# A diffusion block on one Trainium2 core: the attention's value projections emitted between the heads of the delta rule's convolutions

## The chip, the core and the metric

The kernel runs on one NeuronCore of one Trainium2 chip. The engines named below are the matrix engine (PE, whose weight loads the profile lists apart as PEld), the vector engine (DVE), the scalar engine (ACT), GpSimd (POOL) and the queue that issues all DMAs (SP). The metric is the device time of one execution in microseconds. Three executions of the kernel before took 1300.95, 1306.34 and 1319.71 us, so the median is 1306.34 us.

## What is computed

Two layers work on 256 latent tokens (`x`) and 256 context tokens (`ctx`), 1024 wide. In each layer one input projection feeds two mixers: a neighbourhood attention with 8 heads of 64, and a gated delta rule with 4 heads of 128 that runs forwards and backwards over chunks. Both are joined by an output projection, and a squared-ReLU MLP follows. Cut to what matters here:

```python
nq, nk, nv, qkv, z, beta_raw, a_raw = jnp.split(h_lat @ w_in, cuts, axis=-1)      # and the same for the context
na_lat = neighbourhood_attention(heads(nq), heads(nk), heads(nv), ck_h, cv_h, rpb, rows)   # needs nv
q, k, v, beta, g = gdn_inputs(qkv, beta_raw, a_raw, conv_w, a_log, dt_bias, rope)  # conv of width 5, silu, l2norm
o_f, _ = gated_delta_chunked(q, k, v, g[:, :, 0], beta[:, :, 0], s_f)              # holds unit_lower_inverse(a)
y_lat = jnp.concatenate([na_lat, gated_rmsnorm(o_f + flip(o_b), z, gdn_norm_w)], axis=-1) @ w_out
```

The attention needs its values `nv` only when it multiplies by them. Nothing of the delta rule reads them.

## The kernel before

All 512 tokens are held on chip, and the weights stream in as 128x1024 blocks of 512 KB. A product of float32 quality is made of three matmuls on rounded halves (`mm3`, lines 274 to 276), so a weight block is first split: ACT writes the high half `whi` (line 248), DVE subtracts to get the low half `wlo` (line 250). `getw` hands out the blocks in the fixed sequence of `weight_order`, which is derived from the same strings as the program below; three split blocks are kept ahead.

The work of a layer's mixer is written as a string of letters, `CFG["ord0"]` and `CFG["ord1"]`, and `run_order` turns each letter into a call:

- `H` is `gdn_head`: three projections of a delta-rule head (tile `psg`, 24 matmuls each), each followed by the convolution on DVE (line 531, four instructions), a transpose to tokens (`gtr`, line 538); then norms, with a power on POOL (line 229), a scaling on DVE (line 567), and a transpose back (`gtb`, line 570).
- `N` is `proj_nv`: one value projection of two attention heads (tile `psv`, 24 matmuls), a copy on ACT (`vT`), four transposes on PE (`pvt`, line 588) and a copy on ACT into `nv`. On DVE it needs one `wlo`.
- `K` and `Q` are `proj_qk`: the key and query projections of two attention heads (tile `psn`, 24 matmuls each), split on ACT and DVE (lines 744 to 754). `a` is `attend`: scores (`pss`, lines 695 and 696), softmax, transposes (line 713) and the product with `nv` (line 716).
- `f` is `fill`: two of 36 steps of the modulation vectors (tile `adaps`, line 301), each with a DMA of 512 KB of `w_ada`. `Z` is a gate projection (`psz`), `B` and `C` are the decay gates.

At the `X` the function emits the delta rule itself: decay products (line 815), a blockwise triangular inverse by DVE alone (30 pairs at lines 830 and 832, between transposes at 823, 833 and 837), the joining of the blocks by small matmuls on PE (lines 848 to 870; tiles `p1`, `pz`, `p2`, `p3`), and the scan (from line 895). The letters behind `X` are emitted after that.

The letters set priorities only. A list scheduler of the compiler goes through the program, gives each engine its instructions by emission order among those that it holds ready, and fixes one order for each engine; on the chip every engine takes its instructions in that order. So work emitted late (value projections, `K`, `Q`, `a`, `f`) is drawn forward into holes that the scheduler sees on PE in the earlier stages.

Of the kernel before, what the change touches and what calls it, by code (L numbers as in the profile page):

```python
# [37 lines left out]
PAIR2 = True  # L38
KP_OUT = (2, 3, 0, 1)
CFG = {  # L40
    "ord0": "HHBHHCXfNffffNNfffffNKQffaaaKaQfaaKfaQfaffaaKfaQfaZaaaZZfffafffZ",
    "ord1": "BHHHHCNfffXNfffNfNfKfQfaafKfQfaaKfQKfaQfaafffZZZaZ", "tr": 7, "tr2": 2, "acc": 2, "g": 3, "n": 3,
    "late": 3, "tord": (0, 1, 2, 3), "adab": "n", "depth": 3, "npre": 8, "pre1": (0, 2, 3), "vt": "n",
    "tm": 1, "tmh": (2, 3), "gt": 2, "f02": 1, "f12": 2, "f13": 1,
    "start": "WLmmmWme01WLmmmm2eLmbm0mmbLe1m2m0mme12012bb", "cin": 7, "rows": 1,
# [1266 lines left out]
```

## Time and profile before

| | |
|---|---|
| executions shown | 1300.95, 1306.34 and 1319.71 us |
| the profiled execution's own time | 1319.72 us, of which its span is 1317.9 us |
| PE, DVE, ACT busy | 1260.9, 869.5, 594.7 us |
| mixer of layer 0, from its convolutions to its last attention | about 49.5 to 371 us of the span |
| mixer of layer 1 | about 819 to 1093 us |

A stretch of the program is called a stage below: the convolutions (until PE begins the gates' cumulative sums, line 641), the inversion stage (decay products and DVE's inverse, until PE's first `p1`), the block stage (until the first `pvn`, line 895), and scan and rest. Matmuls are pipelined and each is shown until its result is out, so that durations of neighbours overlap: 24 of 0.39 us each can fill 5.7 us.

### The profile page before, as it was taken

Reading aid. Unit: us, or ns where it says so; the run is one execution under the profiler, and the core shown is the slowest. Engines: PE = TensorE matmul, PEld = TensorE weight load, DVE = VectorE, ACT = ScalarE, POOL = GpSimd, SP = SyncE. Lnnn points to the kernel's source line nnn. Section 1 sums busy time; section 2 is a strip of 40 time slices with the busy share of each in tenths; the row PEclk is TensorE's granted clock in tenths of the full one; section 3 lists DMA queues with packets and bytes.
Section 4 is the critical chain, followed back from the end, with each engine's and each line's share of the span. In section 5 each row is a group of like instructions: output and inputs, shape, how many; then the busy total and the mean of one; then the engine's idle time right before and its main releaser. Section 6 shows DMA issues by size and latency. Waiting matters only on the chain.

```text
span 1317.9 us, 20437 instructions
## 1 busy us (share of the span) xinstructions
PE 1260.9 (96%) x7976; PEld 1003.5 (76%) x7976; DVE 869.5 (66%) x1679; ACT 594.7 (45%) x1063; POOL 81.3 (6%) x82
## 2 busy tenths in 40 slices
PE   6999999999999999999999999889989999899997
PEld 3676567877778987777788889665678877788996
DVE  3798795665479954344434588887853658866677
ACT  2555445654446622322322456554353455544542
POOL 0112000000101000000000001230000010000000
PEclk9999998999999999999999999999965999899999
DMA  9514552132165634533532345145710246555552
GB/s 327 207 64 149 179 181 66 45 108 86 61 212 200 212 117 127 158 114 127 158 118 96 112 163 205 61 152 173 237 59 21 89 143 233 188 188 191 180 189 96
DMA packets 62721, 190.93 MB, mean 145 GB/s; under 512 B 7808, under 2 KB 17824, under 8 KB 62624
## 3 DMA queue, kind: packets, MB, share of 16 engines
q1 hardware_dynamic: 62624, 189.62, 43.2%
q8 instruction: 63, 1.03, 0.3%
q14 instruction: 34, 0.28, 0.1%
HBM read 187.46 MB, written 2.13 MB: 144 GB/s over the span
## 4 chain that ended last, share of the span: by engine, by line
PE 74%; DVE 8%; ACT 3%; issue 3%; DMA 2%; POOL 1%; DVEq 0%; SPq 0%; ACTq 0%; POOLq 0%
PE pst L274 8%; PE pst L276 8%; PE pst L275 8%; PE pm L274 7%; PE pm L276 7%; PE pm L275 7%; PE pss L716 3%; PE adaps L301 3%; DMA wraw<-w_ada 2%; DVE wlo L250 2%; PE psn L274 2%; PE psn L275 2%; PE psn L276 1%; PE pss L696 1%; PE pss L713 1%
## 5 line engine op out<-in xcount | busy, mean ns | idle before, releaser
L250 DVE TENSOR_TENSOR wlo<-wraw,whi 128x1024 fp32r<-128x1024 f32 x224 | 272.8, 1220 | 195.1 <-ACT whi L248 194.5
L248 ACT ACTIVATE whi<-wraw 128x1024 fp32r<-128x1024 f32 x224 | 236.8, 1059 | 330.4 <-PE pst L276 169.9
L274 PE MATMUL pm<-hhi,whi 128*128 128x256 f32 (+1 forms) x544 | 176.7, 325 | 0.8 <-ACT whi L248 0.7
L276 PE MATMUL pm<-hhi,wlo 128*128 128x256 f32 (+1 forms) x544 | 175.0, 322 | 0.0
L275 PE MATMUL pm<-hlo,whi 128*128 128x256 f32 (+1 forms) x544 | 174.8, 321 | 0.0
L274 PE MATMUL pst<-whi,ah 128*128 128x512 f32 x384 | 151.9, 396 | 0.0
L275 PE MATMUL pst<-wlo,ah 128*128 128x512 f32 x384 | 151.3, 394 | 0.0
L276 PE MATMUL pst<-whi,al 128*128 128x512 f32 x384 | 151.1, 394 | 0.0
L274 PEld LDWEIGHTS pm<-hhi,whi 128*128 128x128 f32 x544 | 102.4, 188 | 15.2 <-issue 5.8
L276 PEld LDWEIGHTS pm<-hhi,wlo 128*128 128x128 f32 x544 | 102.4, 188 | 8.5
L275 PEld LDWEIGHTS pm<-hlo,whi 128*128 128x128 f32 x544 | 102.5, 188 | 8.1
L274 PEld LDWEIGHTS pst<-whi,ah 128*128 128x128 f32 x384 | 72.3, 188 | 17.1 <-issue 0.8
L276 PEld LDWEIGHTS pst<-whi,al 128*128 128x128 f32 x384 | 72.3, 188 | 16.8
L275 PEld LDWEIGHTS pst<-wlo,ah 128*128 128x128 f32 x384 | 72.3, 188 | 16.4
L274 PE MATMUL psg<-hhi,whi 128*128 128x512 f32 (+1 forms) x216 | 78.1, 363 | 4.0 <-ACT hhi L1067 1.9
L275 PE MATMUL psg<-hlo,whi 128*128 128x512 f32 (+1 forms) x216 | 77.9, 361 | 0.2 <-DVE hlo L1068 0.2
L276 PE MATMUL psg<-hhi,wlo 128*128 128x512 f32 (+1 forms) x216 | 77.3, 358 | 0.4 <-DVE wlo L250 0.4
L531 DVE SCALAR_TENSOR_TENSOR XT<-U,cw,XT 128x512 f32<-128x512 f32 (+1 forms) x96 | 67.0, 726 | 1.8 <-ACT XT L529 1.6
L1190 ACT ACTIVATE ah<-mr 128x256 fp32r<-128x256 f32 (+1 forms) x68 | 33.4, 491 | 66.2 <-DVE mr L1188 66.2
L301 PE MATMUL adaps<-wraw,scT 128*32 128x256 f32 x640 | 55.1, 391 | 3.8 <-DMA wraw<-w_ada 3.6
L274 PE MATMUL psn<-hhi,whi 128*128 128x512 f32 (+1 forms) x128 | 52.5, 410 | 0.0
L229 POOL TENSOR_TENSOR rs<-ve,mh 128x1 f32<-128x1 f32 x12 | 12.2, 1020 | 637.6 <-DVE bmv L394 368.4
(658 smaller groups left out, 2427.4 us busy)
## 6 DMA issues: line engine op xcount, KB each, us to landing
wraw<-w SPq DMA_DIRECT2D x140, 512.0 KB
wraw<-w_ada SPq DMA_DIRECT2D x80, 512.0 KB
wraw<-w_gdn SPq DMA_DIRECT2D x27, 512.0 KB
wraw<-w_out SPq DMA_DIRECT2D x24, 512.0 KB
xa<-w_ada SPq DMA_DIRECT2D x32, 256.0 KB
wraw<-w_vz SPq DMA_DIRECT2D x16, 512.0 KB
wraw<-w_na SPq DMA_DIRECT2D x16, 512.0 KB
lnrow<-lnr SPq DMA_DIRECT2D x8, 512.0 KB
```

The source lines that it names most:

```text
L229: G.tensor_tensor(outp, x, m, op=ALU.pow)
L248: S.activation(hi, r, AF.Copy)
L250: V.tensor_tensor(lo, r, hi.bitcast(F32), op=ALU.subtract)
L274: PE.matmul(o, l[0], r[0], start=start, stop=False)
L275: PE.matmul(o, l[0], r[1], start=False, stop=False)
L276: last_mm[:] = [PE.matmul(o, l[1], r[0], start=False, stop=stop).ins]
L301: PE.matmul(st["ps"][32 * g:32 * g + 32, :256], scT[:, k, :], w[:, 256 * g:256 * g + 256], start=(k == 0), stop=(k == 7), tile_position=(0 ...
L531: V.scalar_tensor_tensor(av, cin[:, sg:, kk:kk + 256], cw[:, b, kk:kk + 1], av, op0=ALU.mult, op1=ALU.add)
L696: PE.matmul(ps[:, :128 * nkt], nqT[hp][hs, a2, qs], nkT[hp][1][hs, :128 * nkt], start=False, stop=True)
L713: PE.transpose(ps[:, 128 * kt_:128 * kt_ + 128], p_[:, 128 * kt_:128 * kt_ + 128], ident)
L716: PE.matmul(ps[:, 0:65], p_[:, 128 * kt_:128 * kt_ + 128], nv[:, kt_, hd], start=kt_ == 0, stop=kt_ == nkt - 1)
L1190: S.activation(ah, r, AF.Copy)
```

## The change

The four `N` of each layer move from behind the gates (`C`) to places right behind the letters `H`. In layer 0 one `f` less stands in the string; the string had more `f` than there are steps, and what is left of the steps is emitted at its end, so the same steps run. No operation is added or removed.

```diff
-    "ord0": "HHBHHCXfNffffNNfffffNKQffaaaKaQfaaKfaQfaffaaKfaQfaZaaaZZfffafffZ",
-    "ord1": "BHHHHCNfffXNfffNfNfKfQfaafKfQfaaKfQKfaQfaafffZZZaZ", "tr": 7, "tr2": 2, "acc": 2, "g": 3, "n": 3,
+    "ord0": "HNHNBHNHNCXfffffffffKQffaaaKaQfaaKfaQfaffaaKfaQfaZaaaZZfffafffZ",
+    "ord1": "BHNHNHNHNCfffXfffffKfQfaafKfQfaaKfQKfaQfaafffZZZaZ", "tr": 7, "tr2": 2, "acc": 2, "g": 3, "n": 3,
```

What it does to the fixed orders of the engines is wider than that. Counted over PE's order of layer 0 (matmuls as the program issues them), stage by stage, before and after:

| layer 0, PE | `psv` | `psn` | `pvt` | `adaps` |
|---|---|---|---|---|
| convolutions | 35, 96 | 0, 4 | 4, 16 | 24, 5 |
| inversion stage | 61, 0 | 86, 137 | 12, 0 | 64, 91 |
| block stage | 0, 0 | 34, 3 | 0, 0 | 8, 0 |
| scan and rest | 0, 0 | 72, 48 | 0, 0 | 32, 32 |

In layer 1 the same counts are `psv` 37 and 96 in the convolutions, 59 and 0 in the inversion stage; `psn` 110 and 140 in the inversion stage, 43 and 4 in the block stage.

The first place is PE at the end of layer 0's convolutions, at the last head's transposes back (`gtb`). Before:

```order
L274 MATMUL psv_2139<-hhi_82,whi_1027 128x512
L301 MATMUL adaps_2030<-wraw_2100,scT_77 32x256 x4
L275 MATMUL psv_2139<-hlo_83,whi_1027 128x512
L276 MATMUL psv_2139<-hhi_82,wlo_1028 128x512
L274 MATMUL psv_2139<-hhi_82,whi_1027 128x512
L275 MATMUL psv_2139<-hlo_83,whi_1027 128x512
L570 MATMUL gtb_1012<-cst_63,ktok3_457 128x128 x4
L570 MATMUL gtb_1019<-cst_63,XT_447 128x128 x4
```

and now:

```order
L276 MATMUL psv_1193<-hhi_82,wlo_1077 128x512
L274 MATMUL psn_2309<-hhi_82,whi_1144 128x512
L275 MATMUL psn_2309<-hlo_83,whi_1144 128x512
L276 MATMUL psn_2309<-hhi_82,wlo_1145 128x512
L274 MATMUL psn_2309<-hhi_82,whi_1144 128x512
L588 MATMUL pvt_1220<-cst_63,vT_1218 128x128 x4
L301 MATMUL adaps_2186<-wraw_2187,scT_77 32x256
L570 MATMUL gtb_1129<-cst_63,ktok3_457 128x128 x4
```

Before, the second of the four value projections was under way at this point; now all four are done, and the first key projection has begun.

The second place is DVE inside layer 0's inverse, whose pairs are lines 830 and 832. Before:

```order
L830 TENSOR_TENSOR btmp<-MY 128x240
L832 TENSOR_TENSOR MY<-MY,btmp 128x15x16
L830 TENSOR_TENSOR btmp<-MY 128x238
L832 TENSOR_TENSOR MY<-MY,btmp 128x14x17
L250 TENSOR_TENSOR wlo<-wraw,whi 128x1024
L830 TENSOR_TENSOR btmp<-MY 128x234
L753 TENSOR_TENSOR KL<-psn,KS 64x512
```

and now:

```order
L745 SCALAR_TENSOR_TENSOR QS<-psn,QS 64x512
L832 TENSOR_TENSOR MY<-MY,btmp 128x22x9
L250 TENSOR_TENSOR wlo<-wraw,whi 128x1024
L830 TENSOR_TENSOR btmp<-MY 128x210
L250 TENSOR_TENSOR wlo<-wraw,whi 128x1024
L832 TENSOR_TENSOR MY<-MY,btmp 128x21x10
L745 SCALAR_TENSOR_TENSOR QS<-psn,QS 64x512
L830 TENSOR_TENSOR btmp<-MY 128x220
```

The queries of the first pair of heads now stand before step 11 of the inverse, where before the first keys came only behind step 17. Over the whole inverse (between the transposes at 823 and 833) DVE's order holds six `wlo` where it held four, four instructions each of lines 745, 753 and 754 where it held two each, and one more each of lines 307 and 710. In the decay products ahead of it there are no `wlo` where there were two. In layer 1 the inverse holds seven `wlo` for six and one more set of instructions for a score.

The third place is PE between the two halves of layer 0's first `p1`, the start of the block stage. Before:

```order
L274 MATMUL psn_2619<-hhi_82,whi_2357 128x512
L275 MATMUL psn_2619<-hlo_83,whi_2357 128x512
L276 MATMUL psn_2619<-hhi_82,wlo_2358 128x512
L301 MATMUL adaps_2261<-wraw_2649,scT_77 32x256 x4
L301 MATMUL adaps_2261<-wraw_2655,scT_77 32x256
L848 MATMUL p1_1308<-XT_447,U_446 32x32 x16
L852 MATMUL pz_1309<-U_446,y1_1307 32x32
```

and now:

```order
L276 MATMUL psn_2820<-hhi_82,wlo_2604 128x512
L848 MATMUL p1_1464<-XT_447,U_446 32x32 x16
L274 MATMUL psn_2820<-hhi_82,whi_2603 128x512
L275 MATMUL psn_2820<-hlo_83,whi_2603 128x512
L276 MATMUL psn_2820<-hhi_82,wlo_2604 128x512
L848 MATMUL p1_1464<-XT_447,U_446 32x32 x16
L852 MATMUL pz_1465<-U_446,y1_1463 32x32
```

Ten matmuls of a key projection and five of `adaps` stood between the halves; three matmuls stand there now.

## Rows read from the trace of the kernel before

**Rows 1.** The page: busy time of each engine; the span in 40 slices.
```profile
PE 1260.9 (96%) x7976; PEld 1003.5 (76%) x7976; DVE 869.5 (66%) x1679; ACT 594.7 (45%) x1063; POOL 81.3 (6%) x82
PEclk9999998999999999999999999999965999899999
```

**Rows 2.** Stages of both layers: stretch, its us, busy us (instructions), clock, DMA.
```profile
core 0: us, PE busy (x) PEld busy (x) DVE busy (x) ACT busy (x) POOL busy (x), PEclk, DMA share, GB/s
49.50:130.20 80.70, 73.39 (x387) 56.36 (x387) 72.29 (x144) 44.23 (x77) 19.78 (x21) 1.00 0.34 113
130.20:194.20 64.00, 60.52 (x364) 40.20 (x363) 51.78 (x108) 28.18 (x63) 3.51 (x1) 1.00 0.55 186
...
231.30:371.00 139.70, 137.99 (x886) 108.57 (x882) 78.23 (x234) 74.21 (x187) 12.32 (x11) 1.00 0.22 74
819.30:888.90 69.60, 61.08 (x356) 48.33 (x354) 61.02 (x138) 37.47 (x71) 17.51 (x20) 0.98 0.33 106
```

**Rows 3.** Waits of PE in the convolutions of layer 0, then of layer 1.
```profile
PE gtb L570 <- DVE ktok L567: 5.5, 4, 1.6
PE gtr L538 <- DVE XT L534: 1.7, 1, 1.7
...
PE gtb L570 <- DVE ktok L567: 4.5, 3, 1.5
PE adaps L301 <- DMA wraw<-w_ada: 1.9, 1, 1.9
PE psg L274 <- ACT XT L529: 1.3, 1, 1.3
PE gtr L538 <- DVE XT L534: 0.5, 1, 0.5
PE psg L276 <- DVE wlo L250: 0.4, 1, 0.4
```

**Rows 4.** One value projection on PE alone, 24 matmuls: us, busy PE, PEld, ACT, clock, DMA.
```profile
115.20:120.90 5.70, 5.70 (x24) 4.39 (x24) 0.00 (x0) 1.00 0.82 283
```

**Rows 5.** Groups on PE in layer 0's convolutions: busy us, mean ns, idle before.
```profile
L301 PE MATMUL adaps<-wraw,scT 128*32 128x256 f32 x48 | 3.8, 387 | 0.0
L588 PE MATMUL pvt<-cst,vT 128*128 128x128 f32 x4 | 0.6, 272 | 0.0
```

**Rows 6.** Groups on DVE in layer 0's inverse, 158.6 to 190 us.
```profile
L830 DVE TENSOR_TENSOR btmp<-MY 128x30 f32<-128x30 f32 (+14 forms) x30 | 9.9, 330 | 0.8
L250 DVE TENSOR_TENSOR wlo<-wraw,whi 128x1024 fp32r<-128x1024 f32 x4 | 4.9, 1221 | 0.2 <-ACT whi L248 0.2
L745 DVE SCALAR_TENSOR_TENSOR QS<-psn,QS 64x512 fp32r<-64x512 f32 x2 | 1.4, 688 | 0.1
L753 DVE TENSOR_TENSOR KL<-psn,KS 64x512 fp32r<-64x512 f32 x2 | 1.4, 684 | 0.0
L754 DVE CAST KS<-KS 64x512 fp32r<-64x512 f32 x2 | 0.8, 423 | 0.1
L825 DVE MEMSET MY<- 128x32 f32 x1 | 0.1, 85 | 1.2 <-ACT MY L824 1.2
```

**Rows 7.** PE in order of time where layer 0's block stage begins.
```profile
194.21 1.19 PE L848 MATMUL p<-XT,U 32*32 32x32 f32 x32 [1.85 <-ACT XT L835]
197.82 1.05 PE L301 MATMUL adaps<-wraw,scT 128*32 128x256 f32 x10
200.87 1.10 PE L848 MATMUL p<-XT,U 32*32 32x32 f32 x29 [2.00 <-ACT y L849]
```

**Rows 8.** The later part of the block stages, all instructions; columns as in Rows 2.
```profile
200.90:231.30 30.40, 30.40 (x546) 23.50 (x547) 15.20 (x37) 15.20 (x28) 0.00 (x0) 0.89 0.18 56
960.00:965.10 5.10, 2.77 (x16) 2.16 (x15) 4.99 (x7) 5.03 (x5) 0.00 (x0) 0.99 0.00 0
965.10:1013.00 47.90, 47.90 (x558) 39.73 (x558) 18.45 (x45) 18.10 (x33) 1.80 (x1) 0.50 0.14 42
```

**Rows 9.** The same two stretches, instructions on `psn` alone; busy PE, PEld, DVE, ACT.
```profile
200.90:231.30 30.40, 9.70 (x24) 5.67 (x24) 2.07 (x3) 1.71 (x3) 0.89 0.18 56
965.10:1013.00 47.90, 10.40 (x28) 6.98 (x28) 2.22 (x4) 1.94 (x4) 0.50 0.14 42
```

**Rows 10.** Stretch of the start with the highest DMA rate; PE's wait for DMA in layer 0's inversion.
```profile
20.00:40.00 20.00, 18.39 (x142) 9.35 (x141) 6.10 (x16) 3.68 (x7) 0.00 (x0) 1.00 1.08 365
...
PE adaps L301 <- DMA wraw<-w_ada: 1.5, 1, 1.5
```

## The prediction

> **What bounds the kernel now.** I read the page first. PE is busy for 1260.9 of 1317.9 us, and the clock line shows full speed nearly everywhere, with one dip to 0.6 and 0.5 in the second layer's mixer [rows 1]. Since the change adds no work, the time can only change through what PE waits for, and through the clock at which its work runs. So I cut the two mixers into stages and read the stretches one by one.
>
> In layer 0's convolutions both PE and DVE are nearly full: 73.4 and 72.3 of 80.7 us [rows 2]. PE waits 7.2 us there, 5.5 of them in four waits of `gtb` (one per head) for DVE's scaling, which itself stands behind a power on POOL [rows 3]. Layer 1 shows the same, with 8.6 us of waits [rows 3]. The reader is to see that there are holes, but that all of them together are half of one layer's moved work. In the inversion stage PE is busy 60.5 of 64.0 us, because projections and modulation steps fill the time in which DVE alone works at the inverse [rows 2]. The inverse itself leaves DVE hardly a gap: its 30 steps and all that stands between them follow each other, and the only large hole is 1.2 us in front of line 825 [rows 6]. The block stage begins with two waits of PE, 1.85 and 2.00 us, for ACT [rows 7], and is then full of PE work [rows 8]. What follows it is PE work without holes: 138.0 of 139.7 us [rows 2].
>
> **The change, step by step.** All sums are made against the profiled execution, 1319.7 us.
>
> *Unit prices.* 24 matmuls of a projection take 5.70 us when nothing disturbs them, so one is 0.238 us [rows 4]. Four `pvt` take 0.6 us, so one is 0.15. 48 records of `adaps` take 3.8 us [rows 5]; the program issues 24 there, so one issued is 0.158 us. A `wlo` is 1.22 us [rows 6].
>
> *Layer 0, convolutions.* PE gets 61 `psv`, 4 `psn` and 12 `pvt` more and 19 `adaps` less: 65 x 0.238 + 12 x 0.15 - 19 x 0.158 = 15.5 + 1.8 - 3.0 = 14.3 us. DVE gets three `wlo` more, 3.7 us, so by DVE the stage would end 3.7 us later and by PE more; PE sets the end. What PE gains is its waits. The first `gtb` comes where it came, since the instructions ahead of it on DVE are the same and PE has no more to do before it. Behind it PE has 74 to 96 projection matmuls per head where it had 53 to 74, and it reaches the later `gtb` after DVE. So I take off three of the four waits: 5.5 less the longest, 1.6, is 3.9. The stage ends **10.4 us later**. The bounds are 7.1 (all waits of PE go) and 14.3 (none goes).
>
> *Layer 0, inversion stage.* PE has 10 projection matmuls less and 27 `adaps` more, 12 `pvt` less: nearly the same work. DVE decides. Its inverse now holds two `wlo` (2.4), two of each of lines 753, 754 and 745 (1.4 + 0.8 + 1.4) and two short ones (0.8) more, 6.8 us [rows 6], and DVE takes its instructions in order, so they delay the steps behind them; `p1` on PE waits for the result. The two keys' instructions in front of line 825 fall into the 1.2 us hole. **5.6 us later**; bounds 0 (they fall into waits that the old trace does not show) and 6.8. The two `wlo` that leave the decay products fill holes there and give nothing back.
>
> *Layer 0, block stage.* Up to 200.9 us DVE and ACT set the pace; with three matmuls for ten between the halves of `p1` PE only waits longer. After that 24 `psn` and three `adaps` are gone, which took 9.7 + 0.5 us of a 30.4 us stretch that was full [rows 8, 9]. They covered the round trips from PE over ACT or DVE and back, of which the one that shows uncovered costs 2.0 us [rows 7]. I let two of these appear: 10.2 - 4.2 = **6.0 us earlier**; bounds 0 and 10.2.
>
> *Layer 0, scan and rest.* 24 `psn` and a few pieces of attention less on a full PE: 5.7 + 1 = **6.7 us earlier**. Layer 0 in all: 10.4 + 5.6 - 6.0 - 6.7 = +3.3.
>
> *Layer 1.* Convolutions: 63 projection matmuls and 12 `pvt` more, 7 `adaps` less: 15.0 + 1.8 - 1.1 = 15.7; here a whole value projection stands in front of the first `gtb`, so all its waits but the 1.3 for ACT go [rows 3]: 7.3 less, **+8.4** (bounds 7.1 and 15.7). DVE's two more `wlo` (2.4) are hidden under that. Inverse: one `wlo` and one score more on DVE, 2.3 at most; **+2** (bounds 0 and 2.3). Block stage: 28 `psn` of 10.4 us are gone, which ran at clock 0.50 [rows 8, 9], and about 2 us of attention; three of that come back as waits: **-9.4** (bounds 0 and -12.4). Rest: five `psn` more, **+1**. Layer 1: +2.0.
>
> *Sum.* 1319.7 + 3.3 + 2.0 = 1325. The profiled execution is 13.4 us slower than the median. [...] Then the sum is +10.0, from the median 1316. Which of the two the median is, one trace can't show; I take the middle, **1320 us**.
>
> *DMA.* No transfer is added. The 512 KB loads of `w_ada` move forward: 91 issued matmuls are 23 loads in layer 0's inversion stage for 16. 186 GB/s over 64 us are 11.9 MB; 3.7 MB more in 69.6 us make 224 GB/s, under the 365 that the start shows [rows 2, 10]. I put nothing on it; it is a rival below.
>
> *A rule weighed.* In the convolutions PE's matmuls are busy 91% of the time and its weight loads 56.4 of 80.7 us, 70% [rows 2]. [...] By that share alone 24 us would be free in the stage, and the value projections would cost only DVE's 3.7. In the stretch where PE runs one projection without a hole, however, the weight loads are 4.39 of 5.70 us, 77% [rows 4]; 70% of 77% is again 91%, so I keep 10.4.
>
> **The rivals.** *PE's clock falls in layer 0's block stage too.* In layer 1 PE was busy 2.77 of 5.10 us at 960 us, and from then to the first `pvn` the granted clock was 0.50; in layer 0, after waits of 1.85 and 2.00 us, it was 0.89 over the stage [rows 7, 8]. [...] Since part is hidden under the new waits I price it at 12: **1332**. [...]
>
> *The convolutions absorb the projections.* If PE has slack that the busy time hides, or if all waits go, DVE sets the end: 3.7 and 2.4 for 10.4 and 8.4, 12.7 less, **1307**, no slower than before. The sum of unit prices speaks against: 251 matmuls at 0.238, the transposes and the waits leave about 3 us of the 80.7. It decides where PE reaches each `gtb` before DVE.
>
> *The loads of `w_ada` come too late.* Such a wait costs 1.5 and 1.9 us [rows 10, 3]; seven loads more in layer 0 and two in layer 1 stand close behind each other, and PE takes them in order between the decay products. Five waits of 1.6: **1328**. The rate above speaks against it.
>
> That the projections stay where they were can't be: PE's fixed order has all four ahead of the last `gtb`.
>
> **How the numbers follow.** Forecast 0.45, 1312 to 1327; clock 0.25, 1328 to 1338; absorbed 0.18, 1299 to 1312; loads 0.12, 1322 to 1334. Together they put about 0.1 below 1303 and 0.1 above 1336, which is the range. 2% of 1306.34 is 26 us, about what a measurement of this kernel can tell from no change. Above 1332.5 lies about half of the clock's case and a quarter of the loads': 0.16. Below 1280 lies 0.03; the rest is 0.81.
>
> **What would show it.** In the profile after, the convolutions of layer 0 should last about 91 us with one large wait at `gtb`; the inverse between lines 825 and 833 about 5 us longer; PE should stand still for over 4 us between the halves of the first `p1`; the stretch from there to `pvn` should be about 24 us, and the clock line tells the second case. The prediction is wrong where the convolutions end within 4 us of before, or where the inverse is no longer than it was.

## The result, and the profile after

The changed kernel takes 1364.79 us (median of four executions, 1361.81 to 1365.54); the kernel before, on the same chip, 1312.94 us. The ratio is 1.04 with a 95% interval of 1.0341 to 1.0459: **slower by 52 us**. The forecast was 1320 us with a range of 1303 to 1336, so the measured time lies 29 us above the range.

The profiled execution's span is 1362.5 us for 1317.9, 44.6 us more. The two lines of the page that answer to [rows 1]:

```profile
PE 1289.3 (95%) x7976; PEld 1023.7 (75%) x7976; DVE 873.0 (64%) x1679; ACT 596.2 (44%) x1063; POOL 83.8 (6%) x82
PEclk9999977599999999999999999999875999899999
```

The same 7976 matmul records are busy for 28.4 us more: the work is the same, so part of it ran slower. The clock line has a new dip, 7 7 5, in layer 0's mixer. The stages of the changed kernel, columns as in [rows 2]: first layer 0's convolutions, inversion stage, block stage, scan and rest, then the same of layer 1.

```profile
49.50:144.90 95.40, 88.32 (x425) 69.48 (x423) 78.75 (x146) 50.28 (x85) 21.80 (x21) 0.98 0.25 81
144.90:220.00 75.10, 68.45 (x404) 40.99 (x403) 55.50 (x116) 27.02 (x60) 3.51 (x1) 0.91 0.66 209
220.00:264.50 44.50, 40.84 (x558) 33.57 (x558) 18.25 (x41) 20.00 (x30) 0.00 (x0) 0.51 0.04 10
264.50:399.20 134.70, 133.13 (x846) 105.39 (x844) 74.84 (x224) 71.44 (x183) 12.24 (x11) 0.97 0.21 70
847.80:931.90 84.10, 76.40 (x420) 61.96 (x420) 66.02 (x141) 43.69 (x80) 19.13 (x20) 0.98 0.27 85
931.90:1009.10 77.20, 64.35 (x410) 39.26 (x410) 56.46 (x127) 29.27 (x64) 3.51 (x1) 0.91 0.63 207
1009.10:1054.30 45.20, 39.30 (x553) 32.88 (x553) 20.18 (x41) 20.41 (x31) 1.80 (x1) 0.50 0.04 10
1054.30:1137.40 83.10, 82.57 (x603) 69.47 (x602) 46.29 (x146) 39.87 (x104) 7.58 (x8) 0.96 0.31 101
```

[rows 2] has four stages of the kernel before; the other four, layer 0's block stage and layer 1's last three, are:

```profile
194.20:231.30 37.10, 35.10 (x598) 26.80 (x599) 21.82 (x42) 21.83 (x32) 0.00 (x0) 0.91 0.18 58
...
888.90:958.40 69.50, 66.50 (x424) 42.92 (x423) 56.15 (x122) 31.40 (x68) 3.51 (x1) 1.00 0.63 203
958.40:1013.00 54.60, 52.25 (x605) 43.39 (x605) 25.05 (x51) 24.73 (x37) 1.80 (x1) 0.56 0.12 37
1013.00:1093.00 80.00, 79.88 (x600) 67.06 (x599) 47.76 (x145) 39.61 (x104) 7.60 (x8) 0.98 0.34 105
```

Layer 0's block stage now runs at a granted clock of 0.51 where it had 0.91, and PE stands for 12.85 us of layer 1's inversion stage (77.20 less 64.35) where it stood for 3.0.

**An account that closes.** Moved work adds nothing to a kernel whose bound is PE. It can only change how long PE stands, and how much of PE's work runs at the lower of the two clocks that these traces show, 0.50 and 1.00 of full speed: cut into slices of 1 us from 8 to 1317 us, the trace before has 70 at 0.50, 1227 at 1.00 and 12 between, the trace after 139, 1152 and 18. So I split each span into three: idle time (span less PE's busy time), half of what PE was busy in the stretches at half clock, and what is left, the work at full clock. The stretches at half clock that matter, and the sum over all of them, in the kernel before:

```profile
965.00:1016.20 51.20, 51.14 (x572) 42.98 (x573) 19.66 (x48) 19.65 (x40) 1.80 (x1) 0.50 0.13 40
...
sum 76.40, PE 69.32 PEld 55.87 DVE 37.32 ACT 29.83 POOL 2.39; mean PE 9.90 PEld 7.98 DVE 5.33 ACT 4.26 POOL 0.34
```

and in the changed kernel (layer 0's inversion stage, its block stage, layer 1's end of the inversion stage with its block stage):

```profile
179.90:193.60 13.70, 11.18 (x43) 5.53 (x44) 8.26 (x17) 3.13 (x6) 0.00 (x0) 0.50 0.64 197
220.90:268.70 47.80, 44.15 (x555) 36.88 (x553) 19.68 (x46) 21.89 (x39) 1.81 (x1) 0.50 0.03 10
...
1002.50:1060.60 58.10, 45.63 (x580) 39.12 (x581) 28.44 (x59) 24.69 (x39) 1.80 (x1) 0.50 0.07 21
...
sum 151.80, PE 125.60 PEld 101.53 DVE 79.55 ACT 58.29 POOL 6.02; mean PE 12.56 PEld 10.15 DVE 7.95 ACT 5.83 POOL 0.60
```

| us | before | after | difference |
|---|---|---|---|
| idle time of PE | 57.0 | 73.2 | +16.2 |
| half of the busy time at half clock | 34.7 | 62.8 | +28.1 |
| the rest: work at full clock | 1226.2 | 1226.5 | +0.3 |
| span | 1317.9 | 1362.5 | +44.6 |

The rest agrees to 0.3 us, so **28 us of the loss are clock and 16 us are PE standing**. By stage the 28 are 5.6 in layer 0's inversion stage, 18.7 about its block stage (44.15 less the 6.8 that two short dips had there before, halved), nothing in layer 1, and some 4 in dips of 3.4 us. The 16 are 3.2 in layer 0's inversion stage, 9.9 in layer 1's, 1.7 and 3.6 in the two block stages, and about -2 in the rest.

This is the split of two single executions. That the clock is lower is no accident of this pair: the mean granted clock over a whole execution was 0.944 to 0.949 in the four of the changed kernel, and 0.961 to 0.988 in those of the kernel before that the experiments were measured against.

What the convolutions didn't give back stands in their waits (us in total, times, longest); these answer to [rows 3], PE's in layer 0, then in layer 1:

```profile
PE gtb L570 <- DVE ktok L567: 5.0, 4, 1.5
...
PE gtb L570 <- DVE ktok L567: 5.9, 4, 1.6
```

and this is the wait of DVE that stands ahead of PE's in layer 0:

```profile
DVE grs L563 <- POOL grs L229: 5.1, 4, 1.6
```

All four waits of layer 0 are still there, 5.0 us for 5.5, and layer 1 has 5.9 for 4.5.

### The profile page after: what moved, and what is told of

Its sections match the earlier page's. It is cut to its first block, busy times and chain, and to the rows that moved or that the text cites. A ratio compares the mean times of both kernels' runs of the same rounds, so it can differ in the third digit from the quotient of the medians.

```text
span 1362.5 us, 20425 instructions
## 1 busy us (share of the span) xinstructions
PE 1289.3 (95%) x7976; PEld 1023.7 (75%) x7976; DVE 873.0 (64%) x1679; ACT 596.2 (44%) x1063; POOL 83.8 (6%) x82
## 3 DMA queue, kind: packets, MB, share of 16 engines
q1 hardware_dynamic: 62624, 189.62, 42.5%
## 5 line engine op out<-in xcount | busy, mean ns | idle before, releaser
L274 PEld LDWEIGHTS pm<-hhi,whi 128*128 128x128 f32 x544 | 102.4, 188 | 15.3 <-issue 5.8
L301 PE MATMUL adaps<-wraw,scT 128*32 128x256 f32 x640 | 59.8, 398 | 0.0
L276 PE MATMUL psn<-hhi,wlo 128*128 128x512 f32 (+1 forms) x128 | 52.2, 408 | 3.9 <-DVE wlo L250 3.9
```

The costliest lines, as they stand in the source:

```text
L274: PE.matmul(o, l[0], r[0], start=start, stop=False)
L276: last_mm[:] = [PE.matmul(o, l[1], r[0], start=False, stop=stop).ins]
L301: PE.matmul(st["ps"][32 * g:32 * g + 32, :256], scT[:, k, :], w[:, 256 * g:256 * g + 256], start=(k == 0), stop=(k == 7), tile_position=(0 ...
```

## The experiments

In the account used below, "idle" and "clock" are the first two rows of the table above for the run's profiled execution. Ratios are to the kernel before on the same chip; the changed kernel's is 1.04. The edits are cut to the lines that matter.

### One layer at a time

```diff
# e1_layer0: the kernel before with the new ord0 alone
+    "ord0": "HNHNBHNHNCXfffffffffKQffaaaKaQfaaKfaQfaffaaKfaQfaZaaaZZfffafffZ",
# e2_layer1: the kernel before with the new ord1 alone
+    "ord1": "BHNHNHNHNCfffXfffffKfQfaafKfQfaaKfQKfaQfaafffZZZaZ",
```

> Layer 0 alone takes the new order; layer 1 keeps the old one. If each layer's loss is made inside its own mixer, this run is slower than before by what the two profiles show between the starts of the two layers, about 28 us: +14 in the convolutions, +11 in the inversion stage, +7 in the block stage at a granted clock of 0.5, -5 in what follows. If the prediction's terms hold and the rest of the loss comes from the two layers disturbing one another (loads, or the clock of one stage carried into another), it is +3.

> Layer 1 alone takes the new order. If each layer's loss is its own, +16 us: +14 in the convolutions, +8 in the inversion stage, -9 in the block stage (which runs at a granted clock of 0.5 in either order), +3 in what follows. By the prediction's terms it is +2. The sum of this run and of the one with layer 0 alone should be the whole loss, about 45, if nothing couples the layers.

Layer 0 alone: 1336.41 us, ratio 1.0199 (1.0147 to 1.0251). Layer 1 alone: 1338.02 us, 1.0217 (1.0157 to 1.0277). Together 24.6 + 26.2 = 51 us is the whole loss, so each layer makes a loss by itself, and no large coupling shows. That the sum fits to 1 us is luck: each interval is some 7 us wide to either side, and the clock of the untouched layer moves by as much. Layer 1's share was expected at 16. Its own stages are as in the changed kernel (83.4, 76.4 and 42.8 us); what is more lies in the untouched layer 0, whose block stage fell to half clock in this execution:

```profile
194.10:241.20 47.10, 46.67 (x598) 35.23 (x598) 22.07 (x42) 21.91 (x32) 0.00 (x0) 0.64 0.15 46
```

The same instructions in the same order took 37.1 us at 0.91 in the trace that I predicted from. In the run with layer 0 alone it is layer 1's untouched block stage that differs, 42.8 us for 54.6. So the kernel before gets more than one clock pattern, and the one trace was no fixed number for either stage. With the old order of layer 0 untouched, its block stage also took 35.5 us at 0.90 (e13) and 47.1 us at 0.64 (e12). The executions of the kernel before over all batches lie between 1300.6 and 1328.7 us.

### Needless matmuls where the clock falls

```diff
# e3_after_fill (changed kernel, 12 per layer), e4_before_fill (kernel before, 8 per layer)
+    with tc.issue_after(p1_):          # behind the first half of the first p1
+        for _ in range(12):
+            PE.matmul(pz, hT[0][:, 0, 0:128], hT[0][:, 1, :], start=True, stop=True)
# e9_after_bigfill (changed kernel): 14 there, and four ahead of each p2 and p3
# e12_before_fill1 (kernel before, layer 1 alone): 14 there, and two ahead of each p2 and p3
```

> The changed kernel with 12 needless matmuls of 128x512 per layer behind the first half of the first p1, on operands that are there and into a tile that is overwritten before it is read: PE's work there is longer by about 12 x 0.24 = 3 us, and PE doesn't stand still between the halves. Nothing is left out of the computation. If the hole at the start of the block stage is what lets the clock fall, layer 0's block stage goes back to a clock near 1 and lasts some 30 us for 44.5, and the time falls by 10 to 14 us in layer 0, and by as much in layer 1 if the clock holds there too. If the clock has fallen for what lies ahead of the block stage (the half-idle inversion stage), the stage stays at 0.5 and the time is the same or 1 to 3 us longer. If the clock were the whole of the loss, the time would come back to within 15 us of before; by the stages' table it can't, since 14 + 11 us of layer 0 lie ahead of that stage.

> The kernel before with 8 such needless matmuls in the same place of both layers. In layer 1 the granted clock was 0.5 from the start of the block stage to the first pvn, 47.9 us. If the hole there is the cause, that stage shortens to 30 to 37 us and the kernel is 10 to 16 us faster than before; layer 0's stage, which was at 0.9, gets at most 2 us longer. If the cause lies ahead of the hole, no change, or 2 to 4 us slower by the work added.

> The changed kernel with 14 needless matmuls of 128x512 behind the first half of the first p1 and four before each p2 and p3 (46 a layer, 10.9 us at 0.238). In the changed kernel the block stage holds three psn and otherwise small matmuls, and runs at a granted clock of 0.5 for 38 us. If it is the missing large matmuls that keep the clock down, it comes back to near 1 within the stage: 38 us of work at half clock are about 20 at full clock, 11 of fill come on top, so the stage lasts 35 to 40 us for 44.5, and the kernel is 5 to 15 us faster than the changed one in spite of the work added. If the clock stays at 0.5 whatever PE does there, the stage lasts about 60 us and the kernel is 25 to 40 us slower.

> The kernel before with 30 needless matmuls of 128x512 in layer 1's block stage alone (14 behind the first half of the first p1, two before each p2 and p3; 7.1 us at 0.238). The account of the traces so far is: span = 1230 us of matmul work at full clock + half of the busy time at half clock + idle time. Before, layer 1's block stage is at half clock for 51 us, which costs about 21. If the fill keeps the clock, that falls to 5 to 10 and the kernel is 4 to 9 us faster than before; if the clock falls at the hole anyway and comes back no earlier, it is 7 to 14 us slower.

e3: 1358.66 us, ratio 1.0362 (1.0307 to 1.0416), not to be told from the changed kernel. The fill shortened PE's wait for ACT in the hole from 3.6 to 0.5 us, the clock came back for 6.8 us and fell again, and the stage lasted 42.4 us for 44.5. The hole alone isn't the cause. e4: 1330.23 us, 1.0138 (1.0069 to 1.0207), a little slower: the scheduler let the eight matmuls take the place of five psn and all five adaps in the hole, so PE waited there as before (2.3 us), and layer 0's stage had a half-clock stretch of 30.7 us.

e9 puts large matmuls through the whole stage. 1361.12 us, 1.0409 (1.0353 to 1.0465): the same as the changed kernel with 92 matmuls more, 21.9 us at 0.238. Layer 0's half-clock stretches are now

```profile
219.90:223.30 3.40, 3.40 (x8) 2.64 (x9) 3.35 (x3) 3.38 (x3) 0.00 (x0) 0.50 0.02 5
240.40:264.30 23.90, 23.90 (x246) 19.29 (x243) 5.41 (x14) 7.36 (x18) 0.00 (x0) 0.50 0.01 1
```

27.3 us for 47.8. The account has 39.6 us of clock for 62.8, and the mean clock was 0.964 to 0.970 in all four executions for 0.944 to 0.949: the fill earned back its own price and no more. Large matmuls in the stage shorten the time at half clock, so the loss of psn there (34 before, 3 after) is part of why it is long; as the clock fell again at 240.4 with PE busy throughout (40.24 of the stage's 40.70 us), they aren't all of it. e12, 1320.60 us, 1.0079 (1.0035 to 1.0124), shortened layer 1's block stage from 54.6 to 37.6 us, but layer 0's fell to half clock in its profiled execution, and the kernel was no faster.

### The waits at `gtb`

```diff
# e5_after_defer, e6_before_defer: gtb emitted behind the next head's first projection
-    PE.transpose(pb[:, t], tk[kind][:, t], ident)        # in gdn_head
+    pend.append((h, kind, q0, tk[kind]))                 # flushed behind the next psg
# e10_after_nopow, e11_before_nopow: no power on POOL
-    rsq(rs, ss, mh.rearrange("p (a b) -> p a b", a=2))
+    V.tensor_scalar(rs, ss, 0.05, None, op0=ALU.min)
# e14_before_split, e15_after_split: the power per projection, as soon as its sums are there
+    V.tensor_scalar(ss[:, kind], ss[:, kind], 4 * NORM_EPS, None, op0=ALU.add)
+    rsq(rs[:, kind], ss[:, kind], mh[:, 0:4])
```

> The changed kernel with the transposes back to channels (gtb) of each head emitted behind the next head's first projection (the last head's behind the gates), so that PE reaches them 15 to 20 projection matmuls, some 4 us, later. The four waits at gtb, 5.0 us in layer 0 and 5.9 in layer 1, should go. If PE's work sets the end of the convolutions and those waits are the whole of the slack, layer 0's stage ends 3.5 to 5 us earlier (from 96 to 91 or 92) and layer 1's 4 to 6 earlier, and the kernel is 8 to 11 us faster than the changed one. If DVE's chain sets the end (its own waits for split weights, 5.9 us, stand in it), the stage doesn't shorten: the waits only move to gtr or psg.

> The same edit on the kernel before, without the change. If PE sets the end there too, 5.5 us of waits go in layer 0 and 4.5 in layer 1: 6 to 10 us faster than before. If DVE, which is busy 72.3 of 80.7 us there, sets the end, no gain.

> The changed kernel with the power on POOL that scales the keys and queries of a head replaced by a small DVE instruction (a minimum with 0.05), so this part of the computation is changed: keys and queries aren't normalised. In the changed kernel DVE waits 5.1 us for that power in layer 0's convolutions, once per head, and PE waits 5.0 us at gtb, once per head. If the round trip over POOL is what keeps PE waiting at gtb, both go, and the convolutions end 4 to 5 us earlier in each layer: 8 to 10 us faster than the changed kernel. If DVE's chain as a whole is late, the wait at gtb or at gtr stays at 5 to 7 us per layer and the gain is under 4 us.

> The same replacement in the kernel before (keys and queries aren't normalised). If the round trip over POOL is the cause, the 5.5 and 4.5 us at gtb go and the kernel is 8 to 10 us faster than before; if DVE's chain as a whole is late, under 4 us.

> The kernel before with the power on POOL issued per projection, the key's as soon as its sums of squares are there, so that its round trip lies under the query's convolution. Same results, one small power and one small addition more per head. If the round trip is what keeps PE at gtb, most of the 5.5 and 4.5 us of waits go in the two layers and the idle time of PE falls from 57 to about 49; at equal clock the kernel is 6 to 9 us faster. If the query's own round trip still sets the wait, idle stays above 54 and the time is the same.

> The same edit on the changed kernel: gtb waits of 5.0 and 5.9 us go for the most part, convolutions of layer 0 end 3 to 5 us earlier (from 96 to about 92), and the kernel is 6 to 10 us faster than the changed one, still 30 or more slower than before.

e5: 1359.64 us, 1.040 (1.035 to 1.045), no gain. Layer 0's `gtb` waits are gone, and PE waits at the next transpose of the chain, `gtr`, instead:

```profile
PE gtr L540 <- DVE XT L536: 6.4, 4, 2.5
PE gtr L540 <- DVE gss L558: 1.7, 1, 1.7
```

The same in e6 (6.7 us at `gtr`): 1331.16 us, 1.0165 (1.0093 to 1.0238), a little slower; the last head's `gtb` came late, and from the gates' cumulative sums to the inverse it took 25.4 us for 19.1. Giving PE more to do ahead of one wait moves the wait along DVE's chain.

e10 takes the round trip over POOL out of that chain (it leaves out the normalisation of keys and queries, as does e11): 1352.87 us, 1.0301 (1.022 to 1.0381). Layer 0's convolutions end 4.1 us earlier, layer 1's last 6.9 us less, and PE's waits in layer 0 are

```profile
PE gtr L538 <- DVE XT L534: 2.2, 2, 1.8
...
PE gtb L570 <- DVE ktok L567: 0.3, 1, 0.3
```

So the wait is one POOL round trip per head, in DVE's fixed order, and more work on PE doesn't hide it. e11 saved as much in the kernel before (idle 48.7 for 57.0). Between e11 and e10, where the waits are gone from both orders, the end of layer 0's convolutions is 17.5 us apart and layer 1's stage 11.2, together 28.7; with the waits in both orders it was 29. The value projections cost as much where there is no wait that they could fill, so they had filled none. e11 was no faster than the kernel before, 1.0037 (0.9997 to 1.0076), as its clock term was 46.3 for 34.7 in the profiled execution. e15, which hides part of the trip with the same computation, brought the changed kernel to 1359.48 us, 1.0336 (1.0277 to 1.0396), idle 69.0 for 73.2, in the direction expected but within the intervals of the two. e14 cut idle to 52.0 and came to 1327.97 us, 1.0082 (1.0033 to 1.0132), 0.8% slower. In its profiled execution layer 0's block stage ran at half clock from beginning to end, with PE full:

```profile
195.30:246.50 51.20, 49.98 (x583) 40.02 (x580) 21.63 (x44) 22.94 (x41) 0.00 (x0) 0.50 0.10 32
```

### The inversion stage

```diff
# e7_after_dummy: four blocks of 24 needless matmuls (D) where the N had stood
+    "ord0": "HNHNBHNHNCXfDffffDDfffffDKQffaaaKaQfaaKfaQfaffaaKfaQfaZaaaZZfffafffZ",
+    if c == "D":
+        ps = acc("psv")
+        for k in range(24):
+            PE.matmul(ps, hT[0][:, k % 8, 0:128], hT[k // 8 % 2][:, k % 8, :], start=k == 0, stop=k == 23)
# e16_after_pin: changed kernel, both layers; e13_pin_q1: kernel before, layer 1;
# e17_split_pin: e14 and e13 together
-    ps = proj_T(w, t0, "psn")
+    with tc.issue_after(first_p1) if (hp, kind) >= (1, 1) else nullcontext():
+        ps = proj_T(w, t0, "psn")
```

> The changed kernel with four needless blocks of 24 matmuls (128x512, operands that are there, results never read, no work for DVE or ACT) at the places in the string that the four value projections left, in both layers. The scheduler then puts 92 of them into layer 0's inversion stage, and 33 psn where the changed kernel has 137; the block stage gets 33 psn back. Theory: the inversion stage is longer because keys, queries and scores, drawn forward in place of the value projections, bring instructions for DVE among the steps of the inverse and leave PE with waits. Then the stage goes back from 75 to 62-66 us in layer 0 and from 77 to 68-71 in layer 1, with a granted clock of 1 throughout, and the kernel is some 10 us faster than the changed one although it does 192 matmuls more. Rival: the stage is longer for the clock or for its loads of w_ada alone; then it stays above 72 us and the kernel is slower by the work added, about 20 us.

> The changed kernel with the projections from the second pair's query on held behind the first half of the first p1 in both layers. Layer 0's inversion stage then has 68 psn where the changed kernel has 137, and its block stage 21 where it has 3; nothing needless is added. If the keys and queries drawn forward lengthen the inverse by their instructions on DVE, DVE's part between the transposes falls from 52 to 42-46 us, and PE stands idle 6 to 10 us more there since nothing takes their place. If large matmuls in the block stage keep the clock, layer 0's block stage comes back above 0.6 for 0.5. In the sum of both the kernel is 5 us faster to 5 us slower than the changed one; if the places of the value projections themselves cause the loss, neither figure moves.

> The kernel before with no needless work: layer 1's projections from the second pair's query on may be issued only behind the first half of the first p1, so that 25 psn stand in the hole of the block stage where 15 stood, and 38 psn leave the inversion stage. If the hole is what lets the clock fall, layer 1's block stage comes back to a clock near 1 and is shorter by 10 to 15 us, and the kernel is 5 to 10 us faster. If the end of the inversion stage, where PE now has less to do, lets it fall, the half-clock stretch only begins earlier and the kernel is the same or up to 10 us slower.

> The kernel before with the power issued per projection and layer 1's projections from the second pair's query on held behind the first p1, so that the first hole of its block stage is filled with work that is due anyway. Idle about 49 as in the run with the split power, clock loss 25 to 32 instead of 32 to 43: 8 to 12 us faster than before. If the held-back projections only move the half-clock time elsewhere, it is as fast as the split power alone.

e7: with matmuls that need nothing from DVE in the places that the value projections left, layer 0's inversion stage is

```profile
145.20:200.30 55.10, 52.11 (x321) 32.24 (x320) 42.02 (x93) 15.88 (x42) 3.51 (x1) 1.00 0.57 187
```

55.1 us for 75.1, at full clock, and layer 1's is 66.0 for 77.2. The inverse between its transposes lasts 32.3 us; it was 40.7 before and 51.9 in the changed kernel. That is what keys, queries, scores and the splitting of their weights cost among its steps. The kernel is no faster, 1365.30 us, 1.0492 (1.0393 to 1.0591): the 192 needless matmuls are 45.7 us of work. But the account shows what they did. All the stretches at half clock of e7's profiled execution are

```profile
sum 79.60, PE 72.07 PEld 56.50 DVE 37.27 ACT 27.36 POOL 3.65; mean PE 8.01 PEld 6.28 DVE 4.14 ACT 3.04 POOL 0.41
```

so its clock term is 36.0 us and its idle time 53.6 (span 1362.7 less 1309.1 busy), for 62.8 and 73.2 in the changed kernel and 34.7 and 57.0 before. Both terms of the loss go when the places that the value projections left are filled with work that needs nothing from DVE, though the convolutions stay as long as in the changed kernel (95.7 us in layer 0). So the loss lies in what stands in the projections' old places (work that DVE has to finish, or nothing), not in the places that they went to.

How much of the 11.2 us is instructions, and how much clock, e5 shows, whose inverse holds the same instructions (a few of them some places earlier or later) and met the full clock. The stretch in e5, then in the changed kernel:

```profile
167.70:214.40 46.70, 43.30 (x256) 27.86 (x255) 42.94 (x93) 14.51 (x21) 0.00 (x0) 1.00 0.73 239
```

```profile
164.00:215.90 51.90, 46.45 (x253) 28.57 (x252) 43.03 (x93) 13.90 (x20) 0.00 (x0) 0.87 0.70 221
```

93 instructions and 43 us of DVE in both. At full clock the inverse is 6.0 us longer than before; the other 5.2 appear where PE runs at half clock (179.9 to 193.6) and behind it: DVE, in its fixed order, waits for scores of the attention, at line 710 in that stretch and at line 718 after it:

```profile
DVE anm L710 <- PE pss L696: 3.8, 2, 3.3
DVE arc L718 <- PE pss L716: 2.9, 2, 2.2
```

The runs with exactly the changed kernel's order there fit: 49.8 us at a clock of 0.93 (e9), 50.2 at 0.90 (e1), 51.9 and 52.6 at 0.87 (e3, e10).

e16: held back behind `p1`, the keys and queries did leave the inverse, which fell to 48.3 us, and the block stages' clock rose to 0.57 and 0.72. But PE then stands: idle is 87.1 us for 73.2, and layer 0's inversion stage reads

```profile
144.90:216.40 71.50, 53.36 (x336) 28.18 (x334) 51.95 (x113) 23.51 (x56) 3.51 (x1) 0.83 0.63 205
```

1383.13 us, 1.0489 (1.0418 to 1.0561). In the profiled execution clock was traded for idle time (48.4 and 87.1 us for 62.8 and 73.2). That one, 1367.57 us, was the fastest of four: the others took about 1383 us at a mean clock of 0.94, under the changed kernel's, so they had the idle time without a gain in clock, and there is no profile of them. e13 does the same to layer 1 of the kernel before: block stage 42.4 us for 54.6, yet 1317.52 us, 1.0033 (0.9989 to 1.0077), no change. e17, 1323.41 us, 1.0063 (1.0025 to 1.0101), adds nothing. No run beat the kernel before.

## Why the prediction was wrong

The sum for the profiled execution was 1325 us, and it took 1364.2. Of the 39 us between them, 10.4 were missed in the two convolutions, 11.2 in the two inversion stages, 13.4 in layer 0's block stage and some 4 in what follows the block stages.

**Convolutions, +10.4 and +8.4; measured +14.7 and +14.5.** The price of the moved work was right: PE's busy time rose by 14.9 and 15.3 us for 14.3 and 15.7. The failed step is "behind it PE has 74 to 96 projection matmuls per head where it had 53 to 74, and it reaches the later `gtb` after DVE". The work between one `gtb` and the next did grow, but the chain that `gtb` waits for doesn't begin at the last `gtb`. It begins at the transposes of the head's query (`gtr`), and behind these PE has the same work in either order: from the second head of layer 0 on, 11 of a value projection's 24 matmuls stand there in the place of `psg`, and the other 13 ahead of it, where they delay the chain along with PE. From the end of the query's `gtr` to `gtb`, second and third head of layer 0, on PE alone (stretch, us, busy PE, clock, DMA), before:

```profile
77.95:83.97 6.02, 4.37 (x21) 1.00 0.25 87
98.86:105.18 6.32, 5.06 (x25) 1.00 0.28 83
```

and now:

```profile
82.14:88.19 6.05, 4.59 (x23) 1.00 0.24 81
109.65:115.68 6.03, 4.59 (x23) 1.00 0.23 87
```

Among these are 18 and 21 projection matmuls before and 19 and 19 now (the rest are transposes and what overlaps the edges). PE ends them before DVE is ready, as before, and layer 0's stage took the whole price: +14.7, where the upper bound was 14.3.

**Layer 0's inversion stage, +5.6; measured +11.1.** The instructions in DVE's order cost what the sum said (6.0 at full clock, by e5). Missing was that DVE now also waits for PE's scores (6.7 us for 0.6), and that PE runs at half clock for 13.7 us of this stage. PE also stands there more often (6.7 us for 3.5); that this is why its clock fell is not shown.

**Layer 0's block stage, -6.0; measured +7.4.** The rival came true: the granted clock was 0.51 for 0.91. I gave it 0.25 and 12 us. The 12 was my estimate from the stretches at 0.50 and 0.89 [rows 8, 9], and no run shows it as a term; about the stage the clock cost 18.7. The step that failed here is the clock: that this stage would keep its 0.89 [rows 8] rested on one trace, and that was a good draw, as e2 and e12 ran the old order of this stage at 0.64 in 47.1 us. The stretch from the second part of `p1` on was to take about 24 us and took 38.0 (226.5 to 264.5). PE stood between the halves of `p1` for 3.6 us for the 2.00 of [rows 7]; over 4 were foretold.

**Layer 0's rest, -6.7; measured -5.0** (134.7 us for 139.7), with a dip of 3.4 us in the clock.

**Layer 1: inversion +2, measured +7.7; block stage -9.4, measured -9.4; rest +1, measured +3.1.** In the inversion stage I let DVE decide and didn't ask what PE would do: 59 `psv` went and only 30 `psn` came. From its first transposes (line 823) to line 833 layer 1's inverse took 52.6 us for 46.7. DVE's own instructions account for 1.6 of that (44.1 us busy for 42.5), waits for the rest, most of them for PE's scores, which were 2.1 us before. PE had no other work left and stood, 8.6 us of it in one wait for the copies on ACT among DVE's last transposes:

```profile
DVE arc L718 <- PE pss L716: 3.4, 2, 2.4
DVE amx L701 <- PE pss L696: 2.8, 2, 2.5
...
PE p L848 <- ACT XT L835: 8.6, 1, 8.6
```

The block stage came out as predicted, and by its terms: PE's work there fell by 13.0 us (12.4 said) and its waits rose by 3.6 (3 said). That it met half clock again was luck; e1 ran the old order of this stage at 0.76. The sum's +10.0, from the median, is 3.3 + 2.0 + 4.7: it takes a gain of 4.7 us for this stage at full clock in place of 9.4. No run shows that term: with its old order the stage met 0.56 in 54.6 us before and 0.76 in 42.8 us in e1, with the new one 0.50 in 45.2 us. In the rest the half-clock stretch reaches 6.3 us into the stage where it reached 3.2.

**The sum.** The terms for work should have added up to nothing over a layer, as no work is added: layer 0's were 14.3 + 0.1 - 10.2 - 6.7 = -2.5, a gain that no mechanism gives. Checked against the account of idle and clock, the forecast said that idle would hardly change and that the clock's part would fall by some 4 us (in layer 1's block stage, 10.4 us for 28 `psn` less the 6.7 that they are at 0.238); they rose by 16.2 and 28.1.

**The loads of `w_ada`** played no part: PE's larger waits in layer 0's inversion stage (2.7, 1.9, 1.2 and 0.8 us) are for DVE and ACT, none for a load, at 209 GB/s for 186. **The share of weight loads** as the measure of PE's headroom was rightly set aside: weight loads took 70% of the convolutions before and 73% now (69.48 of 95.40 us), and the stage absorbed nothing.

**What stays open.** Why the clock falls at the start of the block stage in one execution and not in another of the same order, and what ends the half-clock stretch. In the changed order layer 0's block stage ran at 0.50 to 0.54 in each profiled execution without needless or held-back work in it (the changed kernel, e1, e5, e10, e15); the old order, untouched in layer 0, met 0.90 and 0.91 in two (the kernel before, e13) and 0.64 in two (e2, e12).

## What to carry to other kernels

In a kernel that its matmul engine bounds, price a change of order by idle time and by busy time at half clock; the terms for moved work must cancel, and a sum in which they don't is wrong. A wait that comes from a round trip in another engine's fixed order wasn't hidden here by more work on PE: it moves to the next instruction that depends on the chain (6.4 us at `gtr` in e5 for 5.0 at `gtb`), and goes only with the round trip (0.3 us left in e10). Work that needs nothing from the busy engine (here the value projections during DVE's inverse) is worth most exactly there (with such work in its place again, e7's inversion stage took 55.1 us for 75.1); moved away, it is replaced by work that does need it.

## What the runs showed of the hardware

The clock of 0.50 lasted while PE was full: 51.14 us busy of 51.20 in the kernel before, 49.98 of 51.20 in e14. So in these stretches of mostly small matmuls (32x32 and 64x64 in the joins) a PE that the profile shows as busy was no sign that the clock would rise. With the large matmuls of e9 put between, layer 0's stretches were shorter (23.9 us, 3.4 us, for 47.8).

The same order met either clock in different executions: layer 0's block stage took 37.1 us at 0.91 in the kernel before and 47.1 us at 0.64 in e2. A term that rests on one trace's clock carries that 10 us with it.
